# One copy of the bias rows, four DMAs for a bias tile, and a 144-column band in the pool mixer of a four-layer encoder

## The chip, the core and the metric

The kernel runs on one core of one Trainium2 chip. The metric is the device time of one execution in microseconds. A core has TensorE (PE), VectorE (DVE), ScalarE (ACT), GpSimd (POOL) and SyncE (SP), each with its own list of instructions, and 16 DMA engines that all queues share. Matmuls write to PSUM; everything else lives in SBUF, and the weights and tables are read from HBM.

## What is computed

The reference is an encoder of four layers over 512 tokens of 1024 features, in fp32. Each layer is a mixer and a gated feed-forward network (FFN), each behind an RMS norm and added to the stream. The mixers are, in order, a Hyena convolution, window attention, a pool mixer and a Hyena convolution again. Two parts matter here, cut short:

```python
def window_attention(xn, w_qkv, q_gain, k_gain, sink, w_o, rel_table):
    ...
    rel = j - BLOCK - a                       # a: row of a block of 128, j: one of 3 * 128 keys
    bias = rel_table[t5_bucket(rel)]          # one value per distance and head, 16 heads
    logits = jnp.where(mask, logits + bias, -1e30)
    ...

def pool_mixer(xn, w_grp, b, scale):
    for g, w in enumerate((2, 4, 8, 16)):     # one window for each group of 256 features
        r = w // 2
        # mean of xn over tokens t - r ... t + r, cut at the ends, less xn itself
        outs.append(mean - xf[..., g * 256:(g + 1) * 256])
    y = jnp.einsum('blgc,gcd->blgd', d, w_grp).reshape(B, L, D) + b
    return y * scale

def swiglu(xn, wg, wu, wd):
    return (jax.nn.silu(xn @ wg) * (xn @ wu)) @ wd
```

## The kernel before, in words

The stream `x` stays in SBUF as eight tiles of 128 features x 512 tokens. A product in fp32 is made of three matmuls in a faster format: both operands are split into a high and a low part, and `mm3` (lines 202 to 204) adds high x high, high x low and low x high. Such matmuls, of 128 x 128 weights and 512 columns, are most of the program. The pool mixer's matmuls (line 999) and the transposes are plain fp32 instead, and the profile counts two instructions, or passes, for each.

Weights come through `wload` (line 176): SP starts a DMA into `raw` (line 181, two buffers), ScalarE casts it to `hi` (line 187), VectorE subtracts to get `lo` (line 188). `hi` and `lo` have five buffers each. SP's list is in order, and a load is started when its `raw` buffer is free. In an FFN's first half, each pair of output blocks takes two `raw` tiles of `in_ff_w_gate` and two of `in_ff_w_up`, and each `raw` tile gives two `hi` and two `lo` tiles.

A scheduler orders each engine's list by priorities, so code order and list order differ, and a tile with more buffers can change what comes first.

The relative bias of attention depends only on the distance. `bias_rows` (line 837) makes one line of 512 values for each of 16 heads, and POOL copies each line 128 times into the DRAM tensor `rows` with four DMAs, one for four heads (line 852). `load_bias` (line 855) reads a tile of 128 query rows x 2 heads x 384 keys from it with one POOL DMA (line 858) whose partition stride is one element short of a row, so that each partition sees its line shifted by one. There are eight such tiles in three buffers; VectorE adds them to the logits (line 880). `bias_rows` and the second Hyena's sine features (`filter_features`) are the side work `early` (line 830): FFN 0 takes one step of it after each pair of output blocks from the second pair on.

The pool mixer (`pool`, line 963) transposes the stream to token blocks `xt` (line 955) and multiplies them with a band matrix: for each of eight tiles `k` of features, four blocks of 128 output tokens. A block needs its own tokens (`near`), and the last or first eight tokens of its neighbours (`far`, all zeros but for an edge): two terms for the blocks at both ends and three for the two between, ten matmuls of 128 columns for a `k` (line 999). `near` and `far` are `band` and `edge` scaled by each token's norm, on VectorE (lines 985 to 987); POOL clears the `far` tiles (line 978). ScalarE writes the result as the high part `ghs` (line 1002), VectorE the low part `gls` (line 1003), both in a strided order; the tiles `mm` of PSUM have four buffers. Then come the group products with `in_pl_w` (lines 1012 to 1015) and FFN 2.

In a Hyena block, `in_proj` makes scaled copies `cw` and `cb` of the short convolution's weights (lines 589 to 592).

Of the kernel before, what the change touches and what calls it, by code (L numbers as in the profile page):

```python
# [10 lines left out]
F32 = mybir.dt.float32  # L11
F32R = mybir.dt.float32r
AF = mybir.ActivationFunctionType
ALU = mybir.AluOpType
# [4 lines left out]
P = 128  # L19
D = 1024  # L20
KD = D // P
# [9 lines left out]
NKV = 4  # L31
GS = 256
NG = D // GS
HY_EMB = 33
FW = 64
NEG = -1e30
WB = (2, 5)
UB = 8
JOBS = [(0, 0), (0, 1), (1, 0), (0, 2), (1, 1), (0, 3), (1, 2), (1, 3)]
# [14 lines left out]
def constants():  # L54
    f32 = np.float32
    c = {}
    f = np.arange(P)
    s = np.arange(P)
    fwd = np.zeros((P, 2, R, P))
    inv = np.zeros((P, R, 2, P))  # L60
    for r in range(R):
        n = ((2 * f[None, :] + 1) * (4 * s[:, None] + r)) % 2048
        a = n * (PI / 1024)
        fwd[:, 0, r] = np.cos(a)
        fwd[:, 1, r] = np.sin(a)
        inv[:, r, 0] = np.cos(a).T / 512
        inv[:, r, 1] = np.sin(a).T / 512
    c["dft_fwd"] = fwd.astype(f32)
    c["dft_inv"] = inv.astype(f32)
    c["dft_neg"] = np.stack([-fwd[:, 1, 1], -fwd[:, 0, 3]], 1).astype(f32)  # L70
    cc = np.arange(L)
    tpm = 4 * (cc % P) + cc // P
    bands = (HY_EMB - 1) // 2
    t = (np.arange(L, dtype=f32) / f32(L - 1)).astype(f32)
    ft = np.linspace(1e-4, bands - 1, bands).astype(f32)
    ang = (f32(2.0 * PI / L) * np.arange(L, dtype=f32))[:, None] * ft[None, :]
    z = np.concatenate([t[:, None], np.cos(ang), -np.sin(ang)], axis=1).astype(f32)
    c["zfeat"] = np.ascontiguousarray(z[tpm].T)
    d0, d1 = math.log(1e-2) / 1.5, math.log(1e-2) / 0.3
    deltas = np.abs(np.linspace(d0, d1, D).astype(f32))  # L80
    dec = np.exp((-t[:, None] * deltas[None, :]).astype(f32)).astype(f32)
    c["decay"] = np.ascontiguousarray(dec.reshape(P, R, D))
    rel = np.arange(4 * P) - (2 * P - 1)
    n = np.abs(rel)
    nf = np.maximum(n, 1).astype(f32)
    large = 8 + (np.log(nf / f32(8)) / f32(math.log(128 / 8)) * f32(8)).astype(np.int32)
    large = np.minimum(large, 15)
    buck = np.where(rel > 0, 16, 0) + np.where(n < 8, n, large)
    oh = np.zeros((33, 4 * P), f32)
    near = n <= P  # L90
    oh[buck[near], np.nonzero(near)[0]] = 1.0
    oh[32, ~near] = NEG
    c["bonehot"] = oh
    pb, pe = np.zeros((P, 4, NB, P)), np.zeros((P, 4, 16))
    for g, w in enumerate((2, 4, 8, 16)):
        r = w // 2
        tt = np.arange(L)
        cnt = np.minimum(tt + r + 1, L) - np.maximum(tt - r, 0)
        m = (np.abs(tt[:, None] - tt[None, :]) <= r) / cnt[None, :] - np.eye(L)
        for n in range(NB):  # L100
            pb[:, g, n] = m[n * P:(n + 1) * P, n * P:(n + 1) * P]
        pe[:, g, :8] = m[0:P, P:P + 8]
        pe[:, g, 8:] = m[P:2 * P, P - 8:P]
    c["poolband"] = pb.astype(f32)
    c["pooledge"] = pe.astype(f32)
    return c


class Kernel:
# [17 lines left out]
    def setup(self):  # L127
# [5 lines left out]
        self.aux = ctx.enter_context(tc.tile_pool(name="aux", bufs=2, space=PSUM))  # L133
        self.dr = ctx.enter_context(tc.tile_pool(name="dr", bufs=1, space=DRAM))
        self.x = [self.tl(per, [P, L], f"x{k}") for k in range(KD)]
        self.ghs = self.tl(per, [P, KD, L], "ghs", F32R)
        self.gls = self.tl(per, [P, KD, L], "gls", F32R)
        self.gh = [self.ghs[:, k] for k in range(KD)]
# [1 line left out]
        self.ident = self.tl(per, [P, P], "ident")  # L140
        with self.tc.high_priority(offset=10000):
            make_identity(nc, self.ident)
        self.ones = self.tl(per, [P, 1], "ones")
        nc.gpsimd.memset(self.ones, 1.0)
        self.mean1 = self.tl(per, [P, 1], "mean1")
        nc.gpsimd.memset(self.mean1, 1.0 / D)
        self.root = self.tl(per, [P, 1], "root")
        with self.tc.high_priority(offset=30000):
            self.sqrt_ready(self.mean1)

# [414 lines left out]
    def in_proj(self, hp, s, g, part):  # L565
# [19 lines left out]
        if part < 2:  # L585
            rn = self.rn[s][g][:, part]
            cw0, cb0 = cw, cb
            cw = self.tl(hp, [P, 3, n], "cw")
            cb = self.tl(hp, [P, n], "cb")
            nc.vector.tensor_tensor(cw, cw0, rn.unsqueeze(1).broadcast_to([P, 3, n]), op=ALU.mult)  # L590
            nc.vector.tensor_tensor(cb, cb0, rn, op=ALU.mult)
        taps = []
# [244 lines left out]
    def bias_rows(self, pool):  # L837
# [9 lines left out]
        line = self.tl(pool, [NH, L], "line")  # L847
        nc.scalar.copy(line, ps[0:NH])
        yield
        self.rows = self.dr.tile([NH, P, L], F32, tag="rows", name="rows")  # L850
        for h in range(0, NH, 4):
            nc.gpsimd.dma_start(self.rows[h:h + 4], line[h:h + 4].unsqueeze(1).broadcast_to([4, P, L]))
            yield

    def load_bias(self, ap, g, e):
        bias = self.tl(ap, [P, 2, 3 * P], "bias", bufs=3)
        h0 = 4 * g + 2 * e
        self.nc.gpsimd.dma_start(bias, bass.AP(self.rows.tensor, self.rows.offset + h0 * P * L + P - 1,
                                               [[L - 1, P], [P * L, 2], [1, 3 * P]]))
        return bias  # L860

    def scores(self, ap, g, n, e):
# [99 lines left out]

    def pool(self, ahead):
        nc, t = self.nc, self.t
        self.pool_ss = self.tl(ahead, [P, 2, NB], "ss")
        bs = self.tl(ahead, [P, KD], "bs")
        nc.vector.tensor_tensor(bs, self.pl_b, self.pl_s, op=ALU.mult)
        with self.tc.high_priority(offset=AHEAD):
            xt = [self.pool_turn(ahead, 0)]
        with self.tc.tile_pool(name="pool", bufs=2) as pp, self.tc.tile_pool(name="pool1", bufs=1) as p1:  # L970
            band = self.tl(p1, [P, 4, NB, P], "band")
            edge = self.tl(p1, [P, 4, 16], "edge")
            near = [self.tl(p1, [P, 4, P], f"near{n}") for n in range(NB)]
            far = [self.tl(p1, [P, 2, 4, P], f"far{n}") for n in range(NB)]
            nc.sync.dma_start(band, t["poolband"])
            nc.sync.dma_start(edge, t["pooledge"])
            for n in range(NB):
                nc.gpsimd.memset(far[n], 0.0)
            xt.append(self.pool_turn(p1, 1))
            ss = self.tl(p1, [P, NB], "st")  # L980
            nc.vector.tensor_tensor(ss, self.pool_ss[:, 0], self.pool_ss[:, 1], op=ALU.add)
            rs = self.rsqrt(ss, [P, NB], p1)
            for n in range(NB):
                f = rs[:, n:n + 1]
                nc.vector.tensor_scalar(near[n], band[:, :, n], f, None, op0=ALU.mult)
                nc.vector.tensor_scalar(far[n][96:P, 0, :, 0:8], edge[96:P, :, 0:8], f[96:P], None, op0=ALU.mult)
                nc.vector.tensor_scalar(far[n][0:32, 1, :, P - 8:], edge[0:32, :, 8:], f[0:32], None, op0=ALU.mult)
            for k in range(KD):
                ps = self.tl(self.mm, [P, L], "mm")
                c, g = slice(k % 4 * P, (k % 4 + 1) * P), k // 2  # L990
                x = xt[k // 4]
                for n in range(NB):
                    terms = [(x[n][:, c], near[n][:, g])]
                    if n:
                        terms.append((x[n - 1][:, c], far[n - 1][:, 0, g]))
                    if n < NB - 1:
                        terms.append((x[n + 1][:, c], far[n + 1][:, 1, g]))
                    for q, (w, v) in enumerate(terms):
                        nc.tensor.matmul(ps[:, n * P:(n + 1) * P], w, v, start=q == 0, stop=q == len(terms) - 1)  # L999
                src = ps.rearrange("p (s r) -> p s r", r=R)  # L1000
                gain = self.g_mix(2, k)
                nc.scalar.activation(self.natural(self.gh[k]), src, AF.Copy, scale=gain)
# [83 lines left out]
```

## Time and profile before

| | us |
|---|---|
| median of 3 runs | 2515.93 |
| lowest and highest run | 2515.85, 2518.41 |
| the profiled execution | 2522.24 |
| its span, first to last instruction | 2520.5 |
| TensorE busy | 2424.2 (96%) |
| VectorE busy | 1478.0 (59%) |
| ScalarE busy | 966.6 (38%) |
| POOL busy | 62.5 (2%) |
| mean granted clock of TensorE | 0.984 |

The order of the program in the span is: Hyena until about 390 us, FFN 0 until about 770, attention until about 1050, FFN 1, the pool mixer from 1464 to about 1506, FFN 2, the second Hyena and FFN 3. Busy time of TensorE is modelled from its pipelined matmuls, so it says when TensorE had work, not how well it was used. The chain of work that ended last is the list of what each step was released by, from the last instruction back. DMA share is the mean busy share of the 16 DMA engines; the granted clock is given as a share of 2.4 GHz.

### The profile page before, as it was taken

The page shows a single profiled execution, that of the slowest core. Times are in us where ns is not written, and L with a number is a line of the kernel's source. Part 1 is how long each engine was busy: PE and PEld are TensorE (multiplying, and loading weights), DVE is VectorE, ACT ScalarE, POOL GpSimd, SP SyncE. Part 2 cuts the span into 40 slices and gives each one's busy share as a digit, 9 for nine tenths or more (in the row PEclk, how much of TensorE's full clock was granted, in tenths as well). Part 3 has the DMA queues.
Part 4 walks back from the last instruction along what each step waited for, and adds up shares of the span by engine and source line. Part 5 has one row for each costly group of instructions (what it writes and reads, how often), then busy time and mean ns, then how long its engine had stood idle before and what let it go on. Part 6 is the DMA issues. An engine that isn't in the chain of part 4 may idle for free.

```text
span 2520.5 us, 29516 instructions
## 1 busy us (share of the span) xinstructions
PE 2424.2 (96%) x11062; PEld 1971.7 (78%) x11062; DVE 1478.0 (59%) x2487; ACT 966.6 (38%) x1771; POOL 62.5 (2%) x161
## 2 busy tenths in 40 slices
PE   7999989699998989999999989999989999999999
PEld 5778877487887778888888777888878888888887
DVE  7989885246334688654443354444338998544432
ACT  5543333133333567543332353333225443433321
POOL 0210000000000011000000000000000000000000
PEclk9999999799999999999999999999999999999999
DMA  4343224733333222233333223333232332333332
GB/s 149 127 158 109 76 67 97 116 92 92 92 100 105 68 93 91 84 92 92 92 94 99 88 64 92 93 97 95 93 133 84 101 101 67 92 95 98 92 94 98
DMA packets 180195, 243.42 MB, mean 97 GB/s; under 512 B 10977, under 2 KB 139633, under 8 KB 177876
## 3 DMA queue, kind: packets, MB, share of 16 engines
q1 hardware_dynamic: 174996, 234.17, 30.0%
q0 software_dynamic: 5056, 7.37, 2.2%
q8 instruction: 87, 1.43, 0.2%
q14 instruction: 56, 0.46, 0.1%
HBM read 218.41 MB, written 23.07 MB: 96 GB/s over the span
## 4 chain that ended last, share of the span: by engine, by line
PE 92%; DVE 3%; DMA 3%; ACT 2%; issue 1%; SPq 0%; ACTq 0%; DVEq 0%
PE mm L202 16%; PE mm L203 16%; PE mm L204 16%; PE aux L204 10%; PE aux L202 10%; PE aux L203 10%; PE aux L424 2%; DMA raw<-in_ff_w_gate 2%; PE aux L702 2%; PE aux L653 1%; PE aux L699 1%; PE mm L914 1%; PE aux L644 1%; PE aux L645 1%; PE mm L999 1%
## 5 line engine op out<-in xcount | busy, mean ns | idle before, releaser
L188 DVE TENSOR_TENSOR lo<-raw,hi 128x512 fp32r<-128x512 f32 x700 | 484.9, 694 | 763.3 <-ACT hi L187 756.1
L187 ACT CAST hi<-raw 128x512 fp32r<-128x512 f32 x700 | 434.2, 621 | 1095.7 <-PE mm L203 662.3
L202 PE MATMUL mm<-ghs,hi 128*128 128x512 f32 x1168 | 470.5, 405 | 28.0 <-ACT hi L187 23.8
L204 PE MATMUL mm<-ghs,lo 128*128 128x512 f32 x1168 | 468.9, 402 | 0.0
L203 PE MATMUL mm<-gls,hi 128*128 128x512 f32 x1104 | 444.8, 403 | 0.0
L202 PEld LDWEIGHTS mm<-ghs,hi 128*128 128x128 f32 x1168 | 222.4, 191 | 86.9 <-ACT hi L187 27.9
L204 PE MATMUL aux<-ghs,lo 128*128 128x512 f32 x704 | 279.5, 397 | 1.2 <-DVE lo L188 1.2
L202 PE MATMUL aux<-ghs,hi 128*128 128x512 f32 x704 | 279.4, 397 | 0.0
L203 PE MATMUL aux<-gls,hi 128*128 128x512 f32 x704 | 279.1, 396 | 0.0
L204 PEld LDWEIGHTS mm<-ghs,lo 128*128 128x128 f32 x1168 | 221.9, 190 | 53.1 <-DVE lo L188 0.5
L203 PEld LDWEIGHTS mm<-gls,hi 128*128 128x128 f32 x1104 | 210.2, 190 | 51.3 <-issue 2.1
L204 PEld LDWEIGHTS aux<-ghs,lo 128*128 128x128 f32 x704 | 132.6, 188 | 35.1 <-DVE lo L188 2.9
L203 PEld LDWEIGHTS aux<-gls,hi 128*128 128x128 f32 x704 | 132.6, 188 | 32.1
L202 PEld LDWEIGHTS aux<-ghs,hi 128*128 128x128 f32 x704 | 132.6, 188 | 32.0
L203 PE MATMUL mm<-hl,hi 128*128 128x512 f32 x352 | 137.4, 390 | 0.0
L203 PE MATMUL aux<-hl,hi 128*128 128x512 f32 x352 | 137.4, 390 | 0.0
L202 PE MATMUL mm<-hh,hi 128*128 128x512 f32 x352 | 137.3, 390 | 0.0
L202 PE MATMUL aux<-hh,hi 128*128 128x512 f32 x352 | 137.2, 390 | 0.0
L204 PE MATMUL aux<-hh,lo 128*128 128x512 f32 x352 | 136.9, 389 | 0.0
L204 PE MATMUL mm<-hh,lo 128*128 128x512 f32 x352 | 136.9, 389 | 0.0
L292 DVE TENSOR_TENSOR t<-aux,rstd 128x512 f32<-128x512 f32 x88 | 60.4, 687 | 64.0 <-PE aux L204 64.0
L296 ACT CAST hh<-t 128x512 fp32r<-128x512 f32 x88 | 54.6, 620 | 109.8 <-DVE t L293 109.8
(276 smaller groups left out, 3492.0 us busy)
## 6 DMA issues: line engine op xcount, KB each, us to landing
raw<-in_ff_w_gate SPq DMA_DIRECT2D x88, 512.0 KB
raw<-in_ff_w_up SPq DMA_DIRECT2D x88, 512.0 KB
raw<-in_ff_w_down SPq DMA_DIRECT2D x88, 512.0 KB
raw<-in_hy_w_in SPq DMA_DIRECT2D x48, 512.0 KB
kd<-k SPq DMA_DIRECT2D x32, 512.0 KB
kt<-kd SPq DMA_DIRECT2D x16, 1024.0 KB
raw<-in_hy_w_out SPq DMA_DIRECT2D x16, 512.0 KB
raw<-in_at_w_qkv SPq DMA_DIRECT2D x12, 512.0 KB
```

Of the source, the lines that this page charges most:

```text
L187: nc.scalar.copy(hi, raw[:, k:k + step])
L188: nc.vector.tensor_tensor(lo, raw[:, k:k + step], hi.bitcast(F32), op=ALU.subtract)
L202: mm(ps, ah, bh, start=first, stop=False)
L203: mm(ps, ah, bl, start=False, stop=False)
L204: mm(ps, al, bh, start=False, stop=last)
L292: nc.vector.tensor_tensor(t2, u[e], rstd, op=ALU.mult)
L296: nc.scalar.copy(a, t2)
L424: nc.tensor.matmul(po[:, ty, e], w, ab[:, r, e], start=m == 0, stop=m == 1)
L644: mm(ps[:, j, e], fwd[:, e, j], u[:, j], start=e == 0, stop=False)
L645: mm(ps[:, j, e], f2(e, j), u[:, 2 + j], start=False, stop=e == 1)
L653: mm(ps[:, j, e], fwd[:, e, r0 + j], u[:, r0 + j], start=e == 0, stop=e == 1)
L702: mm(y[:, e, r * P:(r + 1) * P], v[:, e * P:(e + 1) * P], w, start=st, stop=sp)
```

## The change

It makes five edits. `rows` gets 35 copies of a line instead of 128, all heads by one DMA. A bias tile is read by four DMAs of 32 partitions, since a shift of 32 is reached by starting one copy further on and 32 columns earlier. The band matrix of a token block is 144 columns wide (136 at both ends): its 128 tokens and eight on each side. Each token block is multiplied once per `k`, and its columns overlap those of its neighbours in PSUM, where they add up; the bank is started by the first block alone. The scaled band is written over the band itself. `cw` and `cb` get four buffers instead of the pool's default. The small setup tiles move to the front of the permanent pool, and `ss` and `bs` of the pool mixer join them.

```diff
-    pb, pe = np.zeros((P, 4, NB, P)), np.zeros((P, 4, 16))
+    pb = np.zeros((P, NB, 4, P + 2 * EDGE))
...
         for n in range(NB):
-            pb[:, g, n] = m[n * P:(n + 1) * P, n * P:(n + 1) * P]
-        pe[:, g, :8] = m[0:P, P:P + 8]
-        pe[:, g, 8:] = m[P:2 * P, P - 8:P]
+            a, b = max(n * P - EDGE, 0), min(n * P + P + EDGE, L)
+            o = n * P - EDGE
+            pb[:, n, g, a - o:b - o] = m[n * P:(n + 1) * P, a:b]
...
-            cw = self.tl(hp, [P, 3, n], "cw")
-            cb = self.tl(hp, [P, n], "cb")
+            cw = self.tl(hp, [P, 3, n], "cw", bufs=4)
+            cb = self.tl(hp, [P, n], "cb", bufs=4)
...
-        self.rows = self.dr.tile([NH, P, L], F32, tag="rows", name="rows")
-        for h in range(0, NH, 4):
-            nc.gpsimd.dma_start(self.rows[h:h + 4], line[h:h + 4].unsqueeze(1).broadcast_to([4, P, L]))
-            yield
+        self.rows = self.dr.tile([NH, COPIES, L], F32, tag="rows", name="rows")
+        nc.gpsimd.dma_start(self.rows, line.unsqueeze(1).broadcast_to([NH, COPIES, L]))
+        yield
...
-        self.nc.gpsimd.dma_start(bias, bass.AP(self.rows.tensor, self.rows.offset + h0 * P * L + P - 1,
-                                               [[L - 1, P], [P * L, 2], [1, 3 * P]]))
+        for a in range(P // STEP):
+            o = self.rows.offset + (h0 * COPIES + a) * L + P - 1 - a * STEP
+            self.nc.gpsimd.dma_start(bias[a * STEP:(a + 1) * STEP],
+                                     bass.AP(self.rows.tensor, o, [[L - 1, STEP], [COPIES * L, 2], [1, 3 * P]]))
...
-            band = self.tl(p1, [P, 4, NB, P], "band")
-            edge = self.tl(p1, [P, 4, 16], "edge")
-            near = [self.tl(p1, [P, 4, P], f"near{n}") for n in range(NB)]
-            far = [self.tl(p1, [P, 2, 4, P], f"far{n}") for n in range(NB)]
+            band = self.tl(p1, [P, NB, 4, P + 2 * EDGE], "band")
             nc.sync.dma_start(band, t["poolband"])
-            nc.sync.dma_start(edge, t["pooledge"])
-            for n in range(NB):
-                nc.gpsimd.memset(far[n], 0.0)
...
             for n in range(NB):
-                f = rs[:, n:n + 1]
-                nc.vector.tensor_scalar(near[n], band[:, :, n], f, None, op0=ALU.mult)
-                nc.vector.tensor_scalar(far[n][96:P, 0, :, 0:8], edge[96:P, :, 0:8], f[96:P], None, op0=ALU.mult)
-                nc.vector.tensor_scalar(far[n][0:32, 1, :, P - 8:], edge[0:32, :, 8:], f[0:32], None, op0=ALU.mult)
+                nc.vector.tensor_scalar(band[:, n], band[:, n], rs[:, n:n + 1], None, op0=ALU.mult)
...
                 for n in range(NB):
-                    terms = [(x[n][:, c], near[n][:, g])]
-                    if n:
-                        terms.append((x[n - 1][:, c], far[n - 1][:, 0, g]))
-                    if n < NB - 1:
-                        terms.append((x[n + 1][:, c], far[n + 1][:, 1, g]))
-                    for q, (w, v) in enumerate(terms):
-                        nc.tensor.matmul(ps[:, n * P:(n + 1) * P], w, v, start=q == 0, stop=q == len(terms) - 1)
+                    o = n * P - EDGE
+                    a, b = max(o, 0), min(n * P + P + EDGE, L)
+                    nc.tensor.matmul(ps[:, a:b], x[n][:, c], band[:, n, g, a - o:b - o], start=n == 0,
+                                     stop=n == NB - 1, skip_group_check=True)
```

`EDGE` is 8, `STEP` is 32 and `COPIES` is 128 / 32 - 1 + 32 = 35.

POOL's list from the copy into `rows` on, before (`kl` and `v` are tiles of attention's keys and values, `x4` is four alike in a row):

```order
77 L852 DMA rows<-line_3252 512x1x512 x4
78 L734 MEMSET kl_1074_5531 64x1024
79 L734 MEMSET kl_1075_5532 64x1024
80 L858 DMA bias_5547<-rows 128x2x384
81 L858 DMA bias_5549<-rows 128x2x384
82 L811 COPY v_5524<-q_1119_5747 128x256
83 L811 COPY v_5524<-q_1121_5752 128x256
84 L811 COPY v_5524<-q_1123_5757 128x256
85 L858 DMA bias_6184<-rows 128x2x384
86 L811 COPY v_5524<-q_1125_5762 128x256
```

The same place of the changed kernel:

```order
77 L855 DMA rows<-line_3254 560x1x512
78 L738 MEMSET kl_1076_5530 64x1024
79 L738 MEMSET kl_1077_5531 64x1024
80 L863 DMA bias_5546<-rows 32x2x384 x4
81 L863 DMA bias_5551<-rows 32x2x384 x4
82 L863 DMA bias_6189<-rows 32x2x384 x4
83 L815 COPY v_5523<-q_1121_5752 128x256
84 L815 COPY v_5523<-q_1123_5757 128x256
85 L815 COPY v_5523<-q_1125_5762 128x256
86 L815 COPY v_5523<-q_1127_5767 128x256
```

One DMA stands for four at the copy, and the third bias tile has moved ahead of all copies of `v`.

TensorE's list at the head of the pool mixer, before; `mm_11263` is the PSUM tile of the first `k`:

```order
5235 L999 MATMUL mm_11263<-near_2350_11180,xt_2337_11141 128x128
5236 L999 MATMUL mm_11276<-near_2350_11180,xt_2337_11141 128x128
5237 L999 MATMUL mm_11263<-far_2355_11185,xt_2340_11150 128x128
5238 L999 MATMUL mm_11263<-near_2351_11181,xt_2340_11150 128x128
5239 L999 MATMUL mm_11263<-far_2354_11184,xt_2337_11141 128x128
5240 L999 MATMUL mm_11263<-far_2356_11186,xt_2343_11159 128x128
5241 L999 MATMUL mm_11263<-near_2352_11182,xt_2343_11159 128x128
5242 L999 MATMUL mm_11263<-far_2355_11185,xt_2340_11150 128x128
5243 L999 MATMUL mm_11263<-far_2357_11187,xt_2346_11168 128x128
5244 L999 MATMUL mm_11263<-near_2353_11183,xt_2346_11168 128x128
```

And in the changed kernel, two of its eight `k`:

```order
5235 L990 MATMUL mm_11262<-band_11199,xt_2337_11162 128x136
5236 L990 MATMUL mm_11262<-band_11199,xt_2340_11171 128x144
5237 L990 MATMUL mm_11262<-band_11199,xt_2343_11180 128x144
5238 L990 MATMUL mm_11262<-band_11199,xt_2346_11189 128x136
5239 L990 MATMUL mm_11269<-band_11199,xt_2337_11162 128x136
5240 L990 MATMUL mm_11269<-band_11199,xt_2340_11171 128x144
5241 L990 MATMUL mm_11269<-band_11199,xt_2343_11180 128x144
5242 L990 MATMUL mm_11269<-band_11199,xt_2346_11189 128x136
```

Ten matmuls of 128 columns for a `k` have become four of 136 or 144, and the first `k` needs all four scaled parts of the band before the second begins.

## Rows read from the trace of the kernel before

**Rows 1.** The page: busy time of each engine, and the chain by engine.
```profile
PE 2424.2 (96%) x11062; PEld 1971.7 (78%) x11062; DVE 1478.0 (59%) x2487; ACT 966.6 (38%) x1771; POOL 62.5 (2%) x161
...
PE 92%; DVE 3%; DMA 3%; ACT 2%; issue 1%; SPq 0%; ACTq 0%; DVEq 0%
```

**Rows 2.** Windows of FFN 0: sum, PE, PEld, DVE, ACT, POOL busy; PEclk, DMA share, GB/s.
```profile
445.00:450.00 5.00, 3.95 (x17) 2.83 (x15) 0.00 (x0) 0.00 (x0) 0.00 (x0) 1.00 1.01 114
...
455.00:465.00 10.00, 0.00 (x0) 0.00 (x0) 0.00 (x0) 0.00 (x0) 0.00 (x0) 0.50 1.01 122
```

**Rows 3.** DMA view, 420 to 490 us: queues, and an issue with its landing.
```profile
q0 software_dynamic: 4160, 4.22, 63.2%
q1 hardware_dynamic: 3648, 3.62, 16.8%
...
rows<-line POOLq DMA_DIRECT2D x4, 1024.0 KB, 49.0
```

**Rows 4.** Timeline of POOL and of SP: start, duration, what, idle before.
```profile
427.19 4.51 POOL L852 DMA_DIRECT2D rows<-line  x4 [124.44 <-ACT line L848]
...
430.50 6.00 SPq L181 DMA_DIRECT2D raw<-in_ff_w_gate  x2
```

**Rows 5.** Timeline of ScalarE in FFN 0, the two late casts.
```profile
468.54 0.62 ACT L187 CAST hi<-raw 128x512 fp32r<-128x512 f32 x1 [33.17 <-DMA raw<-in_ff_w_gate]
...
479.43 1.14 ACT L187 CAST hi<-raw 128x512 fp32r<-128x512 f32 x2 [8.71 <-DMA raw<-in_ff_w_gate]
```

**Rows 6.** Timeline of TensorE in FFN 0: both waits, and matmuls behind them.
```profile
469.21 0.79 PE L202 MATMUL mm<-ghs,hi 128*128 128x512 f32 x1 [20.26 <-ACT hi L187]
...
472.70 0.39 PE L204 MATMUL mm<-ghs,lo 128*128 128x512 f32 x1
...
476.21 0.39 PE L204 MATMUL mm<-ghs,lo 128*128 128x512 f32 x1
480.11 0.80 PE L202 MATMUL mm<-ghs,hi 128*128 128x512 f32 x1 [3.50 <-ACT hi L187]
...
486.24 0.40 PE L204 MATMUL mm<-ghs,lo 128*128 128x512 f32 x1
```

**Rows 7.** The chain in the pool mixer: start, duration, what.
```profile
1476.17 19.25 PE mm L999 x156
```

**Rows 8.** Timeline of ScalarE and VectorE in the pool mixer.
```profile
1486.52 1.16 ACT L1002 ACTIVATE ghs<-mm,vec 128x512 fp32r<-128x512 f32 x1 [1.07 <-PE mm L999]
...
1474.13 0.49 DVE L985 TENSOR_SCALAR near<-band,rs_r 128x512 f32<-128x512 f32 x1
...
1489.95 1.12 DVE L1003 SCALAR_TENSOR_TENSOR gls<-mm,vec,ghs 128x512 fp32r<-128x512 f32 x1 [1.12 <-ACT ghs L1002]
```

**Rows 9.** Timeline of TensorE in the first Hyena: fp32 passes of 256 columns.
```profile
301.31 1.03 PE L699 MATMUL aux<-c4a,inv 128*128 128x256 f32 x4
302.17 1.03 PE L699 MATMUL aux<-c4a,ni 128*128 128x256 f32 x4
```

**Rows 10.** Timeline of TensorE: the stage's first matmuls, and the first fast ones.
```profile
1474.77 1.19 PE L999 MATMUL mm<-near,xt 128*128 128x128 f32 x4 [5.29 <-DVE near L985]
...
1479.29 0.49 PE L999 MATMUL mm<-near,xt 128*128 128x128 f32 x2
```

**Rows 11.** Source line of the bias DMA, and VectorE's first use of the last tile.
```profile
L858 POOL DMA_DIRECT2D bias<-rows x8: 708/712/747, 782.8 to 996.8; - x8
...
DMA to landing us min/median/max: 3.5/3.9/8.2
...
1007.91 0.48 DVE L880 CUSTOM_DVE_ANT_0 lg<-mm,bias,vec 128x256 f32<-128x256 f32 x1 [0.30 <-PE mm L878]
```

**Rows 12.** Window behind the second pair of bias DMAs, columns as in rows 2.
```profile
792.00:796.00 4.00, 2.27 (x9) 2.21 (x10) 1.54 (x3) 0.95 (x1) 0.00 (x0) 0.68 0.01 3
```

**Rows 13.** Windows of both Hyena tails, columns as in rows 2.
```profile
330.00:345.00 15.00, 8.49 (x33) 6.41 (x32) 15.00 (x21) 0.62 (x1) 0.00 (x0) 0.77 0.07 26
...
2050.00:2150.00 100.00, 100.00 (x487) 82.90 (x486) 89.57 (x135) 40.74 (x71) 0.80 (x12) 1.00 0.23 75
```

More of the change, by code (lines that the diff above doesn't have):

```diff
@@ L33 @@
 NG = D // GS
+EDGE = 8
 HY_EMB = 33
@@ L36 @@
 NEG = -1e30
+STEP = 32
+COPIES = P // STEP - 1 + STEP
 WB = (2, 5)
@@ L100, in constants @@
         for n in range(NB):
-            pb[:, g, n] = m[n * P:(n + 1) * P, n * P:(n + 1) * P]
-        pe[:, g, :8] = m[0:P, P:P + 8]
-        pe[:, g, 8:] = m[P:2 * P, P - 8:P]
+            a, b = max(n * P - EDGE, 0), min(n * P + P + EDGE, L)
+            o = n * P - EDGE
+            pb[:, n, g, a - o:b - o] = m[n * P:(n + 1) * P, a:b]
     c["poolband"] = pb.astype(f32)
-    c["pooledge"] = pe.astype(f32)
     return c
@@ L135, in setup @@
         self.x = [self.tl(per, [P, L], f"x{k}") for k in range(KD)]
+        self.ones = self.tl(per, [P, 1], "ones")
+        self.mean1 = self.tl(per, [P, 1], "mean1")
+        self.root = self.tl(per, [P, 1], "root")
+        self.pool_ss = self.tl(per, [P, 2, NB], "ss")
+        self.pool_bs = self.tl(per, [P, KD], "bs")
         self.ghs = self.tl(per, [P, KD, L], "ghs", F32R)
@@ L142, in setup @@
             make_identity(nc, self.ident)
-        self.ones = self.tl(per, [P, 1], "ones")
         nc.gpsimd.memset(self.ones, 1.0)
-        self.mean1 = self.tl(per, [P, 1], "mean1")
         nc.gpsimd.memset(self.mean1, 1.0 / D)
-        self.root = self.tl(per, [P, 1], "root")
         with self.tc.high_priority(offset=30000):
@@ L964, in pool @@
         nc, t = self.nc, self.t
-        self.pool_ss = self.tl(ahead, [P, 2, NB], "ss")
-        bs = self.tl(ahead, [P, KD], "bs")
+        bs = self.pool_bs
         nc.vector.tensor_tensor(bs, self.pl_b, self.pl_s, op=ALU.mult)
```

## The prediction

> **What bounds the kernel now.** I read the chain of work that ended last first: 92% of the span is TensorE [rows 1], so a change pays where TensorE stands still, or where it does less work. The places to look at are therefore the stretches in which its busy time falls short of the window. Two of them touch this diff.
>
> The first is in FFN 0. Between 445 and 450 us TensorE runs out of work, from 455 to 465 it does nothing at all, and the 16 DMA engines are full in both stretches [rows 2]. In the 70 us around it the software queue, which only carries the four copies into `rows`, takes 63.2% of all 16 engines; the hardware queue with the weights takes 16.8% [rows 3]. The copies are issued from 427.19 us, a pair of weight loads at 430.50 us [rows 4], and ScalarE's cast of the next weights then waits 33.17 us and 8.71 us for them [rows 5]. TensorE lives on the casts already made, then waits 20.26 us and 3.50 us, each followed by a stretch in which a matmul starts every 0.43 us instead of every 0.234 [rows 6]: the granted clock, at full from 445 to 450, has fallen to 0.50 while TensorE stood still [rows 2], that is 1.2 GHz of 2.4.
>
> The second is the pool mixer: the chain shows 19.25 us of one matmul line [rows 7]. TensorE is the bound there: ScalarE's cast of each result takes 1.16 us and waits 1.07 us for it, so one comes every 2.23 us [rows 8].
>
> **Rows: 4 copies to 1.** The 4.22 MB of the software queue took 0.632 x 70 = 44.2 us of 16 engines [rows 3], 5.96 KB per engine and us. The new copy is 16 x 35 rows of 2 KB = 1.147 MB: 12.0 us of 16 engines at that rate. Begun about 429 us (two us behind its issue), it ends at about 441. Two weight loads of 512 KB stand beside it; the hardware queue moved 3.62 MB in 0.168 x 70 = 11.8 us, so 1.7 us each. The first pair has landed by about 445, even if the copy goes ahead of both. TensorE's stored weights last until 469.21 - 20.26 = 449.0, so the cast and split (1.3 us) are in time, with some 2 us to spare. The whole stall goes: 20.26 + 3.50 of waiting, and of the slow matmuls (472.70 - 469.21) - 8 x 0.234 = 1.6 and (486.24 - 480.11) - 14 x 0.234 = 2.9 [rows 6], together **28.3 us**. No more can go; 20 if the copy moves at 0.6 of the old rate and 6 to 8 us of waiting stay. What is late next is nothing new: weight loads two deep, as in every other FFN pass. POOL issues one copy instead of four, 3 us less, on an engine with nothing else there.
>
> The side work of FFN 0 has three steps less, so the sine features of the second hyena come three passes earlier. Their DVE and ScalarE steps only move; TensorE is the bound of every pass once the stall is out. I cost this at 0, at most +1.
>
> **Pool mixer.** Removed: 80 - 32 = 48 matmuls, 8 of 12 scalings on VectorE, 4 memsets (on POOL, beside TensorE's transposes) and a small DMA. An fp32 matmul is two passes. Twenty passes of 128 columns take 2.23 us [rows 8], so 0.112 each. Passes of 256 columns take 0.86 / 4 = 0.215 [rows 9]; between the two lies 0.81 ns per column, so 136 columns take 0.118 and 144 take 0.125. One k (2 x 136 and 2 x 144 columns, two passes each) is 4 x 0.118 + 4 x 0.125 = 0.97 us, against 2.23. Eight of them at full clock would save 10.1 us, but two things move.
>
> VectorE's first scaling still begins at 1474.13, but TensorE needs all four before k0 is done. A scaling of 512 columns takes 0.49 us [rows 8]; 576 at the same rate take 0.55, so the fourth ends near 1476.3, and k0 near 1476.7. The clock was low when the stage began, and matmuls came at twice the time until 1479.29 [rows 10]; with the same recovery k1 ends at 1478.6, k2 at 1479.9, k3 at 1480.9. Then casts of 1.16 us on ScalarE and 1.12 us on VectorE [rows 8] return the four PSUM buffers about as fast as TensorE fills them, and k7 ends near 1484.7. The group products that begin near 1495.2 (1476.17 + 19.25, less the last pass's drain) now begin there: **10.5 us**. If the clock stayed low throughout, eight k at 1.9 us would end at 1489.9, a gain of 5; were it high at once, the casts would set the end, a gain of 11.5. I take 10.5, from the recovery seen here.
>
> The band is 1.18 MB instead of 1.05, 0.4 us more at the weights' rate; VectorE comes to its first scaling from its own steps, without a wait for the load [rows 8], so this costs nothing.
>
> **Bias tiles: 8 DMAs to 32.** An issue took 0.71 us for 128 partitions and 256 runs, 3.5 to 8.2 us to land [rows 11]. For a quarter of the runs I take 0.43 us, from the copies' 4.51 / 4 = 1.13 us for 512 runs [rows 4] against 0.71 for 256; its bounds are 0.2 and 0.71. So POOL spends between 1 and 17 us more, over eight places, on an engine busy 2% of the span [rows 1]. Queued behind them are additions that VectorE and TensorE don't wait for soon, and the copies of v, with three tiles' DMAs ahead of them instead of two; those need the first third of the q/k/v product, and POOL is idle until it is done. The last tile is the tightest: issued at 996.8, landed at about 1000.7, used at 1007.91 [rows 11], seven us of room for two us of later issues. One thing may show: the third tile's 384 KB are now read at about 786, among weight loads, shortly before a wait of TensorE (2.27 of 4 us busy, [rows 12]). At the rate of that stretch it is 1.3 us; I take +0.3, between 0 and +2.
>
> **The rest.** `cw`/`cb` with four buffers only lets small VectorE steps come earlier; in both hyena tails the scheduler reorders some matmuls around them. In the first tail VectorE is the bound (15.00 of 15 us, TensorE 8.49), and its list is the same; in the second TensorE has no gap to lose (100.00 of 100 us) and each new wait would show [rows 13]. I take +0.2, between -1 and +2. The setup tiles change address only: 0.
>
> **Sum.** -28.3 - 10.5 + 0.3 + 0.2 = -38.3 us. The profiled execution took 2522.24 us (span 2520.5), so its like would be 2483.9; the median of three runs is 2515.93, 6.3 lower. Forecast of the median: 2515.93 - 38.3, rounded **2478 us**.
>
> **Rivals.**
> (a) *The copy is only partly out of the way.* It moves at 0.6 of the old rate, or weights queue behind all of it: 7 us of the stall stay, 2485. For: the weight loads of 430.50 came behind nearly all of the old copies. Against: the margin above.
> (b) *The pool stage stays at the low clock or at the pace of the casts*, and gains 5 to 8: 2481 to 2484. For: the clock dropped in each wait seen here, and k0 now has pauses for its scalings.
> (c) *POOL and VectorE get in each other's way*: 24 more issues, each of which holds up or waits for a VectorE step, in a stage where TensorE has gaps already [rows 12]: at most 24 x 0.71 = 17 us; half of it gives 2486. Against: the eight issues last 0.708 to 0.747 us, next to a busy VectorE, and show no such wait [rows 11]. The Trainium skill (SBUF — State Buffer, SBUF: two separate sides) has a rule for it: a DMA issued from POOL can't have its descriptors written while VectorE runs in a mode that takes the port the two share. The trace does not bear it out so far.
> (d) *The copy reaches few engines.* The four copies together filled 16; the trace doesn't show how many each of them used. If every weight load has shares on all engines, it waits for the fullest. Were the one copy on four, it would take 192 / 4 = 48 us and end at 477: the stall stays as it was, only the pool's gain is left, 2505. The same comes out if the copies were not what held up the weights.
> (e) *Slower*: the same mechanism, on two engines: 96 us, weights at about 525, a stall of 76 instead of 28, +48 - 10.5: 2553. It decides where the copy ends after about 487, under 3.3 engines. For (d) and (e): one issue in place of four. Against: its source has 16 partitions, each old one had 4. By the Trainium skill (DMA: Bandwidth & Descriptors, Why a DMA increments its semaphore by 16 and not by 1) a transfer takes the largest number of engines up to 16 that divides the slowest dimension of both sides: 4 for an old copy, 16 for the new one. By that rule neither (d) nor (e) occurs, and the sum stands.
>
> **How the numbers follow.** Forecast 0.66 (2473 to 2483), (a) 0.11, (b) 0.10, (c) 0.05, (d) 0.05, (e) 0.03. The range must leave out no more than 0.2: from 2472, where all bounds of the sum are at their best (-28.3 - 11.5 - 1, and 3 us for the runs' own spread), to 2492, where (a), (b) and most of (c) lie. Faster by over 0.2% (5 us, about what a measurement of this kernel can tell from no change) are the forecast and (a) to (d): 0.95, taking some of (d) for a copy on three engines; same 0.02; slower 0.03.
>
> **What would show it.** Right: no wait of ScalarE's cast for `in_ff_w_gate` over 10 us in FFN 0, the software queue's share down to about 12 us of 16 engines, the copy landed within 16 us, granted clock 1.00 from 440 to 480; 64 passes in the pool stage within 10.5 us of its first matmul; no idle time of VectorE that a bias DMA ended. Wrong: a gap of TensorE over 5 us behind the copy, a pool stage over 13 us, or TensorE's loss in the attention stage up by over 3 us.

## The result, and the profile after

The changed kernel takes 2436.36 us (median of four runs, 2435.60 to 2437.68) against 2517.17 us before (four runs, 2515.85 to 2518.87). The ratio is 0.968, with a 95% interval of 0.966 to 0.970. So 80.8 us are gone, where I forecast 38 and allowed 24 to 44. The direction was right; the size lies outside the range, on the good side.

The page of the changed kernel: busy time, the software queue, and the chain by engine, which answer to [rows 1] and, over the whole span, to the first row of [rows 3].

```profile
PE 2366.2 (97%) x10966; PEld 1951.8 (80%) x10966; DVE 1471.9 (60%) x2479; ACT 965.3 (40%) x1771; POOL 66.7 (3%) x178
...
q0 software_dynamic: 1840, 4.29, 1.0%
...
PE 93%; DVE 3%; ACT 2%; issue 1%; DMA 0%; SPq 0%; ACTq 0%; DVEq 0%
```

DMA has left the chain. TensorE is busy 58.0 us less, but the pool mixer's share of that is only some 9. To see where the rest sits, cut the span at the last addition that VectorE makes to the stream in each stage (the ends of the timeline's rows for the additions of an FFN, of attention, of the pool mixer and of a Hyena's out-projection; FFN 3 runs to the end of the span). Each stage's length in the profiled execution, in us:

| stage | before | changed | difference |
|---|---|---|---|
| Hyena 1 | 379.8 | 376.7 | -3.1 |
| FFN 0 | 403.1 | 366.6 | -36.5 |
| attention | 308.9 | 299.5 | -9.4 |
| FFN 1 | 373.6 | 364.5 | -9.1 |
| pool mixer | 43.4 | 33.6 | -9.8 |
| FFN 2 | 369.0 | 360.8 | -8.2 |
| Hyena 2 | 271.3 | 268.8 | -2.5 |
| FFN 3 | 371.3 | 363.3 | -8.0 |

The differences add up to 86.6 us, 6 more than the medians differ by: the profiled execution of before took 5 us more than its median, most of it in attention, which lasts 303 to 305 us in three kernels below that change nothing there but the bias DMAs or the speed of the matmuls.

FFN 0 and the pool mixer are what I had counted on. FFN 1, 2 and 3 contain no edit, and each is 8 to 9 us shorter. TensorE stands still for only 2 to 4 us in each of them, before and after alike, so no wait can have gone. The windows view shows what did, in 100 us of FFN 2 (columns as in [rows 2]), first before, then changed:

```profile
1550.00:1650.00 100.00, 100.00 (x428) 80.38 (x428) 48.31 (x73) 32.77 (x54) 0.00 (x0) 1.00 0.33 92
```
```profile
1550.00:1650.00 100.00, 100.00 (x443) 82.84 (x442) 50.32 (x77) 33.90 (x57) 0.00 (x0) 1.00 0.35 100
```

TensorE is busy for all 100 us at full clock in both, and does 443 matmuls where it did 428. The timeline shows each matmul as long as ever (0.39 to 0.40 us with its drain) but started sooner after the last. Before, in FFN 0's first half and then in its second:

```profile
519.75 0.39 PE L203 MATMUL aux<-gls,hi 128*128 128x512 f32 x1
...
521.86 0.40 PE L203 MATMUL aux<-gls,hi 128*128 128x512 f32 x1
...
699.68 0.39 PE L202 MATMUL aux<-hh,hi 128*128 128x512 f32 x1
...
701.49 0.39 PE L204 MATMUL mm<-hh,lo 128*128 128x512 f32 x1
```

and in the changed kernel:

```profile
519.75 0.39 PE L208 MATMUL mm<-ghs,lo 128*128 128x512 f32 x1
...
521.79 0.39 PE L208 MATMUL mm<-ghs,lo 128*128 128x512 f32 x1
```

Nine starts in 2.11 us are 234 ns each; nine in 2.04 are 227. The second half of an FFN, on `hh` and `hl`, ran at 1.81 / 8 = 226 ns before already. So the kernel before had two speeds for one kind of matmul, and its trace showed both.

**FFN 0's stall** went as forecast. Of the changed kernel, the windows, the DMA view (420 to 490 us, then 425 to 435 us, where this queue is the only one), and the timeline of POOL, SP, ScalarE and VectorE:

```profile
435.00:445.00 10.00, 10.00 (x45) 8.29 (x45) 3.37 (x5) 3.90 (x7) 0.00 (x0) 1.00 0.58 173
445.00:450.00 5.00, 5.00 (x23) 4.13 (x22) 4.14 (x7) 2.20 (x5) 0.00 (x0) 1.00 0.31 93
```
```profile
q0 software_dynamic: 304, 1.15, 15.4%
...
rows<-line POOLq DMA_DIRECT2D x1, 1120.0 KB, 13.5
```
```profile
q0 software_dynamic: 240, 0.97, 94.0%
```
```profile
422.55 0.80 POOL L855 DMA_DIRECT2D rows<-line  x1 [122.46 <-ACT line L852]
...
425.81 5.81 SPq L185 DMA_DIRECT2D raw<-in_ff_w_gate  x2
...
437.66 0.62 ACT L191 CAST hi<-raw 128x512 fp32r<-128x512 f32 x1 [7.17 <-DMA raw<-in_ff_w_gate]
...
438.32 0.69 DVE L192 TENSOR_TENSOR lo<-raw,hi 128x512 fp32r<-128x512 f32 x1 [4.86 <-ACT hi L191]
```

The copy takes 0.154 x 70 = 10.8 us of 16 engines and lands 13.5 us behind its issue. From 425 to 435 us it alone fills 94% of the 16 engines, and the weight loads issued from 425.81 us on move nothing in that time. ScalarE's cast still waits 7.17 us for the weights, against 33.17 [rows 5], and TensorE does not notice: in a run below, with a longer copy, its stored weights last until 450.35 - 6.54 = 443.8 us, and here the next cast and split are done by 439.

**The pool mixer**, timeline of TensorE, ScalarE and VectorE, then two windows:

```profile
1416.75 10.79 PE L990 MATMUL mm<-band,xt 128*128 128x136 f32 x64 [4.96 <-DVE band L982]
1427.29 0.48 PE L206 MATMUL mm<-ghs,hi 128*128 128x512 f32 x1
...
1418.99 1.14 ACT L994 ACTIVATE ghs<-mm,vec 128x512 fp32r<-128x512 f32 x1 [3.90 <-PE mm L990]
1420.86 1.14 ACT L994 ACTIVATE ghs<-mm,vec 128x512 fp32r<-128x512 f32 x1 [0.73 <-PE mm L990]
1422.72 6.04 ACT L994 ACTIVATE ghs<-mm,vec 128x512 fp32r<-128x512 f32 x6 [0.72 <-PE mm L990]
...
1416.12 1.81 DVE L982 TENSOR_SCALAR band<-band,rs_r 128x576 f32<-128x576 f32 x4
```
```profile
1419.00:1421.00 2.00, 2.00 (x10) 2.00 (x10) 0.83 (x1) 1.27 (x2) 0.00 (x0) 0.50 0.00 0
1421.00:1423.00 2.00, 2.00 (x12) 2.00 (x11) 1.24 (x2) 1.27 (x2) 0.00 (x0) 0.57 0.03 8
```

From the first scaling to the first group product are 1427.29 - 1416.12 = 11.2 us, against 1495.2 - 1474.13 = 21.1 before [rows 7, 8]: 9.9 us less. The first results come 1.87 us apart at a granted clock of 0.50 (1.2 GHz), the last six at ScalarE's pace of one per us.

### The profile page after: what moved, and what is told of

The parts are those of the page before. It is cut to its first block, busy times and chain, and to the rows that moved or that the text cites. A ratio compares the mean times of both kernels' runs of the same rounds, so it can differ in the third digit from the quotient of the medians.

```text
span 2433.8 us, 29324 instructions
## 1 busy us (share of the span) xinstructions
PE 2366.2 (97%) x10966; PEld 1951.8 (80%) x10966; DVE 1471.9 (60%) x2479; ACT 965.3 (40%) x1771; POOL 66.7 (3%) x178
## 4 chain that ended last, share of the span: by engine, by line
PE 93%; DVE 3%; ACT 2%; issue 1%; DMA 0%; SPq 0%; ACTq 0%; DVEq 0%
PE mm L206 16%; PE mm L207 16%; PE mm L208 16%; PE aux L208 10%; PE aux L207 10%; PE aux L206 10%; PE aux L428 2%; PE aux L706 2%; PE aux L703 1%; PE aux L657 1%; PE mm L919 1%; PE aux L648 1%; PE aux L649 1%; PE aux L438 1%; PE mm L906 1%
## 5 line engine op out<-in xcount | busy, mean ns | idle before, releaser
L206 PE MATMUL mm<-ghs,hi 128*128 128x512 f32 x1168 | 460.7, 397 | 4.2 <-ACT ghs L515 4.2
L208 PE MATMUL mm<-ghs,lo 128*128 128x512 f32 x1168 | 459.6, 394 | 0.0
L207 PE MATMUL mm<-gls,hi 128*128 128x512 f32 x1104 | 435.6, 395 | 0.0
L208 PE MATMUL aux<-ghs,lo 128*128 128x512 f32 x704 | 274.3, 390 | 1.1 <-DVE lo L192 1.1
L206 PE MATMUL aux<-ghs,hi 128*128 128x512 f32 x704 | 274.3, 390 | 0.0
L207 PE MATMUL aux<-gls,hi 128*128 128x512 f32 x704 | 273.9, 389 | 0.0
L208 PEld LDWEIGHTS mm<-ghs,lo 128*128 128x128 f32 x1168 | 220.1, 188 | 45.5 <-issue 0.4
```

The lines of the kernel that those rows point to most:

```text
L206: mm(ps, ah, bh, start=first, stop=False)
L207: mm(ps, ah, bl, start=False, stop=False)
L208: mm(ps, al, bh, start=False, stop=last)
```

## The experiments

The suspect for the rest was the one edit that I had costed at nothing. Tiles of a pool are laid behind one another, each start rounded up to 32 bytes. Moving five small tiles ahead of `ghs` puts its start at byte 33056 of a partition instead of 32896, and the two tiles that come from another pool move the weights `hi` and `lo` by 64 bytes too. Starts in bytes are those of the compiled programs. Times of a start are means over the starts in the trace that follow each other within 150 to 260 ns. The "remainder" is the start of the moving operand less that of its weights, by 256.

### The edits one by one

**a_move**: the kernel before with the tiles moved (and taken out where they stood), nothing else.

```diff
         self.x = [self.tl(per, [P, L], f"x{k}") for k in range(KD)]
+        self.ones = self.tl(per, [P, 1], "ones")
+        self.mean1 = self.tl(per, [P, 1], "mean1")
+        self.root = self.tl(per, [P, 1], "root")
+        self.pool_ss = self.tl(per, [P, 2, NB], "ss")
+        self.pool_bs = self.tl(per, [P, KD], "bs")
         self.ghs = self.tl(per, [P, KD, L], "ghs", F32R)
...
```

> The kernel before with one edit: the setup tiles ones, mean1, root and the pool mixer's ss and bs stand ahead of ghs and gls, as in the change. Theory (addresses): a matmul of 512 columns on ghs or gls starts every 227 ns instead of 234, a product by an FFN takes some 8 us less, the run takes 2467 to 2476 us; the stall of FFN 0 and the ten matmuls for a k stay as they were. Rival (the faster matmuls come from another edit, or from a state of the chip): 234 ns, 2514 to 2520 us.

Measured: 2479.75 us, 37.6 less than before (2517.31 in this comparison), ratio 0.985 (0.983 to 0.986); a bit slower than my interval. In the trace, TensorE, ScalarE and POOL run the instructions of before in the order of before; VectorE's list differs in one small product, `bs`, which has moved from 1094.9 to 3.2 us. So the order of the work is not what changed the time. Matmuls on `ghs` and `gls` start every 227 ns. In the same 100 us of FFN 2:

```profile
1550.00:1650.00 100.00, 100.00 (x442) 82.79 (x442) 49.35 (x76) 33.27 (x55) 0.00 (x0) 1.00 0.33 95
```

FFN 2 takes 360.8 us, as in the changed kernel. FFN 0 keeps its stall (395.3 us), and the pool mixer its length (43.9).

**b_unmove**: the changed kernel with the same five lines behind `ident`.

> The changed kernel with the five setup tiles back behind ident, so that ghs starts at byte 32896 of a partition again and the weights hi and lo stay where the change has them. Theory (addresses): matmuls on ghs and gls go back to 230 to 234 ns, those on hh and hl stay at 227, 2460 to 2477 us. Rival: 227 ns, 2434 to 2440 us.

Measured: 2468.90 us, 32.5 slower than the changed kernel. Matmuls on `ghs` and `gls` start every 233 ns on the mean, those on `hh` every 227. (In each FFN of this kernel one of the three kinds, `ghs` by `hi`, `gls` by `hi` or `ghs` by `lo`, is at 237 ns and the other two at 231 to 232, and it is not always the same kind.) `hi` lies where the changed kernel has it, so moving `ghs` alone brings the slow starts back. Two windows of this kernel, FFN 2's first and second half:

```profile
1550.00:1650.00 100.00, 100.00 (x431) 80.42 (x430) 48.57 (x74) 33.22 (x56) 0.00 (x0) 1.00 0.33 95
...
1715.00:1815.00 100.00, 100.00 (x443) 82.80 (x442) 29.86 (x44) 25.29 (x41) 0.00 (x0) 1.00 0.31 100
```

**c_rows**: the kernel before with `bias_rows` and `load_bias` of the change, these lines of its diff and the constants they use.

> The kernel before with the edit of rows and load_bias alone. Both theories: FFN 0's stall of 28.3 us goes, 2487 to 2491 us, and matmuls on ghs stay at 234 ns. If the four times as many bias DMAs cost something in the attention stage, 2491 to 2497.

Measured: 2484.66 us, 32.6 less (0.987, 0.985 to 0.988). FFN 0 takes 374.6 us instead of 403.1: 28.5 less. Matmuls on `ghs` stay at the slow pace (429 in the 100 us). The total lies below both intervals that I had given: some 4 us more are gone than FFN 0 accounts for, most of them in attention.

**d_pool**: the kernel before with the band of the change, the diff's lines from `pb = np.zeros` on and those of `pool`, without the moved `ss` and `bs`.

> The kernel before with the pool mixer's band edit alone (ss and bs stay where they were). Both theories: 9 to 11 us less, 2506 to 2509 us, matmuls on ghs at 234 ns and FFN 0's stall as it was.

Measured: 2507.76 us, 9.6 less (0.996, 0.995 to 0.997); the pool mixer takes 33.6 us instead of 43.4.

The three add up to 37.6 + 32.6 + 9.6 = 79.8 of the 80.8 us.

### What about the address

**e_front32, f_mid64, g_mid32**: the changed kernel with an unused tile, ahead of `ghs` or behind `ident`.

```diff
+        self.tl(per, [P, 8], "pad")
         self.ghs = self.tl(per, [P, KD, L], "ghs", F32R)
```
```diff
         self.ident = self.tl(per, [P, P], "ident")
+        self.tl(per, [P, 16], "pad")
```

(8 instead of 16 in g_mid32.)

> The changed kernel with 32 unused bytes ahead of ghs: ghs, hi, lo and hh all move by 32 bytes, and each now starts on a multiple of 64 bytes, as ghs did before; the distance from ghs to hi keeps its remainder of 0 by 256. Theory 1 (the distance between the start of the moving operand and that of the weights, by its remainder of 256, sets the interval: 0 fast, 128 and 160 slow): 227 ns, 2434 to 2440 us. Theory 2 (an operand that starts on a multiple of 64 bytes is slow): 232 to 234 ns on ghs and hh, 2474 to 2490 us.

> The changed kernel with 64 unused bytes behind ident: hi, lo and hh move by 64 bytes, ghs stays. The distance from ghs to hi has the remainder 192, that from hh to hi keeps 0; all start 32 bytes behind a multiple of 64. Theory 1: matmuls on ghs at 229 to 232 ns, on hh at 227, 2450 to 2466 us. Theory 2: all at 227, 2434 to 2440 us.

> The changed kernel with 32 unused bytes behind ident: the distance from ghs to hi has the remainder 224, that from hh to hi 0; ghs starts 32 bytes behind a multiple of 64, hi and hh on one. Theory 1: matmuls on ghs slower than on hh, 228 to 234 ns against 227, 2440 to 2475 us. Theory 2: ghs 227, hh slower.

Measured: 2438.25, 2468.85 and 2469.30 us. In e_front32 everything has moved by 32 bytes, each start is now a multiple of 64, and all stays at 227 ns: theory 2 is out. In f_mid64 and g_mid32 `ghs` did not move, only the weights did, and `ghs` falls to 233 ns while `hh`, which moved along with the weights, stays at 227. What theory 1 had wrong is the size: I expected small remainders to cost little, and 192 and 224 cost as much as 160, so f_mid64 lies above the theory's 2450 to 2466 us. The windows of f_mid64, first and second half of FFN 2:

```profile
1550.00:1650.00 100.00, 100.00 (x430) 80.16 (x429) 48.90 (x75) 33.13 (x55) 0.00 (x0) 1.00 0.32 93
...
1715.00:1815.00 100.00, 100.00 (x443) 82.84 (x442) 29.77 (x44) 25.29 (x41) 0.00 (x0) 1.00 0.31 99
```

**i_cw2**: the changed kernel without `bufs=4` on `cw` and `cb`.

> The changed kernel with two buffers for cw and cb again. They stand ahead of zh and zl, which start 128 bytes earlier: their distance to hi has the remainder 128 by 256 instead of 0. Theory (distance): the out-projection's matmuls on zh and zl at 232 ns instead of 227, a hyena 1 us longer, 2437 to 2441 us. Rival (the buffers matter by the order of the work, or not at all): 227 ns.

Measured: 2436.10 us (2434.02 to 2437.27), no different from the changed kernel's 2436.36, and a little below the theory's 2437 to 2441. Matmuls on `zh` and `zl` start every 232 ns instead of 227, as the theory says; but Hyena 1 ends 1.7 us later and Hyena 2 is 0.4 us shorter, and there are too few of them to show in the time. So the four buffers are worth nothing that can be measured, apart from what their bytes do to their neighbours.

**n_lo64**: the changed kernel with 64 unused bytes between `hi` and `lo`.

```diff
-        self.pending = None
+        self.pending, self.pad = None, True
...
                 hi = self.tl(self.wp, [P, step, ncols], "hi", F32R, bufs=WB[1])
+                if self.pad:
+                    self.pad = self.tl(self.wp, [P, 16], "pad", bufs=1) is None
                 lo = self.tl(self.wp, [P, step, ncols], "lo", F32R, bufs=WB[1])
```

> The changed kernel with 64 unused bytes between hi and lo, so that lo, hh, hl, zh and zl start 64 bytes later and ghs, gls and hi stay. By 256 the distance from ghs and gls to hi has the remainder 0, to lo 192; from hh and hl to hi 64, to lo 0. Three matmuls follow each other: ghs by hi, gls by hi, ghs by lo. Theory 1a (a matmul is slowed by the distance to its own weights): ghs by lo at 233 ns, the other two at 227; hh by hi and hl by hi slow, hh by lo fast. Theory 1b (it is slowed by the distance to the weights that are loaded while it runs, those of the next): gls by hi at 233 ns, the other two at 227; hh by lo and hh by hi slow, hl by hi fast. Some 3280 matmuls at 6 ns more: 2450 to 2460 us by either.

Measured: one run, 2462.34 us, just above the 2450 to 2460 of either form. `ghs` by `lo` is at 235 ns, `ghs` by `hi` at 229 and `gls` by `hi` at 229; `hh` by `hi` at 230, `hl` by `hi` at 229, `hh` by `lo` at 228. The matmul with a remainder to its own weights is the slowest, as in 1a, but its neighbours are no longer at 227, which neither form has. That speaks against 1b, and 1a alone doesn't describe it. One run does not settle it, though: in b_unmove, at one remainder for all, the longest of the three starts fell now on one kind and now on another, so only the mean of the three is safe to read, here 231 ns on `ghs` and `gls` and 229 on `hh` and `hl`. The readings together, as means over the kinds named:

| moving operand, weights | kernel | remainder | ns per start |
|---|---|---|---|
| ghs and gls, hi and lo | before | 160 | 234 |
| the same | changed, a_move, e_front32 | 0 | 227, in Hyena 228 to 229 |
| the same | b_unmove | 96 | 233 (231 to 237 by kind) |
| the same | f_mid64 | 192 | 233 |
| the same | g_mid32 | 224 | 233 |
| hh and hl, FFN 0, 2, 3 | before | 0 | 226 to 227 |
| hh and hl, FFN 1 | before, d_pool, k_bias4 | 64 | 229 (226 to 232 by kind) |
| zh and zl | before, a_move, i_cw2 | 128 | 232 to 233 |
| zh and zl | changed, b_unmove | 0 | 227 to 228 |

### The copy and the bias DMAs

**l_onedma**: the kernel before, its 128 copies by one DMA. **m_copies70**: the changed kernel with twice the copies.

```diff
-        for h in range(0, NH, 4):
-            nc.gpsimd.dma_start(self.rows[h:h + 4], line[h:h + 4].unsqueeze(1).broadcast_to([4, P, L]))
-            yield
+        nc.gpsimd.dma_start(self.rows, line.unsqueeze(1).broadcast_to([NH, P, L]))
+        yield
```
```diff
-COPIES = P // STEP - 1 + STEP
+COPIES = 70
```

> The kernel before with its 128 copies of 16 lines written by one DMA instead of four. Theory (bytes set the time of the copy): TensorE's two waits in FFN 0 together 20 to 28 us, as before, 2512 to 2521 us. Rival (four copies in flight, or four partitions each, are what was slow): the waits under 12 us, 2490 to 2505 us; or one DMA reaches fewer engines and they grow past 40.

> The changed kernel with 70 copies of a line instead of 35, the second half unused. Theory (bytes): the copy lands 25 to 28 us after its issue instead of 13.5, past the 22 us that TensorE's stored weights last, and TensorE waits 4 to 10 us in FFN 0: 2441 to 2450 us. Rival (the number of DMAs counts): no wait, 2434 to 2440 us.

Measured: 2506.84 and 2446.24 us, one run each. TensorE's wait (timeline) and the copy's landing (DMA view, the last figure), first of l_onedma, then of m_copies70:

```profile
468.41 0.80 PE L202 MATMUL mm<-ghs,hi 128*128 128x512 f32 x1 [20.59 <-ACT hi L187]
```
```profile
rows<-line POOLq DMA_DIRECT2D x1, 4096.0 KB, 45.5
```
```profile
450.35 0.80 PE L206 MATMUL mm<-ghs,hi 128*128 128x512 f32 x1 [6.54 <-ACT hi L191]
```
```profile
rows<-line POOLq DMA_DIRECT2D x1, 2240.0 KB, 25.6
```

1120, 2240 and 4096 KB land after 13.5, 25.6 and 45.5 us: 10.7 to 10.8 us for each further 1000 KB, each by one DMA; of the four DMAs of before, 4096 KB in all, the last landed 54.1 us behind the first issue. Bytes set the time of the copy, as the sum had it. With 70 copies the stall is back in part, which also shows how near the edge the margin is: 12 us more on the queue cost 8.4 us of FFN 0 (375.0 against 366.6). In l_onedma the long wait stays, as the theory of bytes says, but the time lies between my two intervals. One DMA instead of four spares the second, smaller wait: FFN 0 takes 396.7 us instead of 403.1. The rest of l_onedma's gain is in attention, of which below; it was timed once.

**k_bias4**: the kernel before, a bias tile read by four DMAs.

```diff
-        self.nc.gpsimd.dma_start(bias, bass.AP(self.rows.tensor, self.rows.offset + h0 * P * L + P - 1,
-                                               [[L - 1, P], [P * L, 2], [1, 3 * P]]))
+        for a in range(4):
+            o = self.rows.offset + (h0 * P + a) * L + P - 1 - a * 32
+            self.nc.gpsimd.dma_start(bias[a * 32:(a + 1) * 32],
+                                     bass.AP(self.rows.tensor, o, [[L - 1, 32], [P * L, 2], [1, 3 * P]]))
```

> The kernel before with a bias tile read by four DMAs of 32 partitions, from the same 128 copies. My price was +0.3 us, between 0 and +2: 2514 to 2520 us. Rival, from the run of rows and bias DMAs together, whose attention stage was 8 us shorter than in the kernel before: the smaller DMAs are what it gains by, 2508 to 2513 us.

Measured: 2515.98 us, ratio 0.9998 (0.9988 to 1.0007). Four times the DMAs cost and gain nothing that can be measured.

That leaves some 4 us of c_rows, most of them in attention. In the kernel before, TensorE has two waits in the q/k/v product:

```profile
813.41 0.49 PE L202 MATMUL mm<-hi,ghs 128*128 128x512 f32 x1 [1.29 <-ACT q L799]
...
819.26 0.41 PE L821 MATMUL aux<-ident,qh 128*128 128x128 f32 x2 [1.23 <-issue]
```

k_bias4, d_pool and a_move have the same two at the same place of the stage (1.3 us each); c_rows, l_onedma and the changed kernel have none over 1.2 us there. What these three share, and the others don't, is one DMA for the copies, and with it three steps less of side work: ScalarE's list then has its first q tile behind 7 casts of attention's weights instead of 8. Attention takes 299.6 and 300.8 us in l_onedma and c_rows, 302.8 and 304.1 in k_bias4 and d_pool, so that order is worth 2 to 4 us. Another part is no effect of any edit: the wait for the norm's sums at the head of the stage was 4.4 us in the profile of before, 2.6 to 2.7 in k_bias4, d_pool, a_move, l_onedma, c_rows and the changed kernel, and 3.9 in e_front32, whose lists of instructions on TensorE, ScalarE and VectorE are the changed kernel's. Between them these make attention 300 to 309 us long.

## Why the prediction was wrong

**The step that failed** is the last sentence of "The rest": "The setup tiles change address only: 0." It measured -37.6 us alone, nearly half of the result. I had asked of each edit which instructions and waits it moves, and this one moves next to none. I had not asked what an address does to TensorE, and the trace of before held the question: 234 ns in [rows 6] next to 226 in FFN 0's second half, for matmuls of one shape at full clock. A term for it could have been worked out: 1168 + 1104 + 1168 + 3 x 704 = 5552 matmuls on `ghs` and `gls`, 7 ns each, 39 us. The trace alone did not say which address would be the good one; beside the compiled starts, its own rows come apart by the remainder (160, 128, 64 and 0 in the table above).

**Rows** were right in FFN 0: 28.3 forecast, 28.5 measured. The price by bytes held over a factor of 3.7. ScalarE's cast still waits 7.17 us, under the 10 that I had allowed, and the margin, put at some 2 us, was 4.8 (443.8 less 439).

**Side work** of FFN 0 did more than move. Three steps less also change the order in attention, for 2 to 4 us less; I had put 0 to +1. **`cw` and `cb`**, put at +0.2, show nothing (i_cw2).

**The pool mixer** gained 9.9 us in the trace and 9.6 in the run of its edit, forecast 10.5. The clock came back later than taken: near 1422.7, 6 us behind the first matmul, where I had put 4.5, and the last six results went at ScalarE's pace. That is rival (b) in mechanism, but the gain lies above its 5 to 8 us.

**Bias tiles**: 0.53 us an issue, forecast 0.43 (the line through the two points that I used gives 0.40); landing 2.2 to 6.4 us. The changed kernel's source line, and the tightest tile (POOL's timeline, and VectorE's first use):

```profile
L863 POOL DMA_DIRECT2D bias<-rows x32: 533/533/562, 743.2 to 950.4; - x32
...
DMA to landing us min/median/max: 2.2/3.6/6.4
```
```profile
948.78 2.12 POOL L863 DMA_DIRECT2D bias<-rows  x4 [12.85 <-DVE m L885]
...
959.87 0.48 DVE L885 CUSTOM_DVE_ANT_0 lg<-mm,bias,vec 128x256 f32<-128x256 f32 x1 [0.30 <-PE mm L883]
```

The price was +0.3 and k_bias4 measured none. Rival (c) did not occur: the 32 issues last 0.533 to 0.562 us next to a busy VectorE. The rule of the Trainium skill (SBUF — State Buffer, SBUF: two separate sides) which (c) drew on, that POOL can't write a DMA's descriptors while VectorE runs in a mode that takes the port they share, shows in none of these issues; whether VectorE ran in such a mode beside one of them is not shown.

**Rivals (a), (d) and (e)** did not occur. Of (a), the weights did queue behind all of the copy, but none of the stall was left. Against (d) and (e), one DMA of 16 partitions fills the 16 engines by itself (94.0% from 425 to 435 us), and in l_onedma it lands its 4096 KB in 45.5 us, against 45.8 to 50.7 for each of the four. By the Trainium skill (DMA: Bandwidth & Descriptors, Why a DMA increments its semaphore by 16 and not by 1) it uses all 16 engines, and the trace agrees.

The range failed with the step. It was built from the bounds of the costed terms, and the one I gave no bounds was the largest. My signs of being right all came but one, and that nearly (64 passes in 10.8 us instead of 10.5): they looked at the costed edits only, so they could not show what was missing.

## What to carry to other kernels

Before calling a matmul-bound stretch full, divide it by the count of its matmuls, and compare that number between stretches of the same shape; busy time says 100% at either speed. An edit that adds, drops or moves a tile, however small, moves what lies behind it, so compare the starts of the hot operands before and after, and time such a move by itself before crediting another edit with its effect. A queue's copy is worth its bytes: count them, and set them against how long the work already loaded will last.

## What the hardware showed that I had not expected

The time from one 128 x 512 matmul to the next depends on where its two SBUF operands start relative to each other. With the starts a multiple of 256 bytes apart it was 226 to 229 ns in the FFN and Hyena products of all kernels here where `hi` and `lo` were both so placed; at remainders of 96, 128, 160, 192 and 224 it was 232 to 234 ns on the mean of the three kinds. Moving both operands by 32 bytes changed nothing (e_front32); moving either alone did (b_unmove, f_mid64). The difference is 3% of such a matmul, and 37.6 us of this kernel in a_move. Three things stay open: why a remainder of 64 cost only 2 ns on the mean (FFN 1 of before), how the three kinds share the loss, and why in n_lo64 also the well-placed matmuls lost 2 ns. What happens inside the engine was not seen; the runs show only which placements are slow. Whether 227 ns can be undercut by another placement was not tried.
